# Laying the head norms of queries and keys in phases in a TensorE-bound hybrid layer

## The chip, the cores and the metric

One core of one Trainium2 chip runs one program. The metric is the device time of one execution in microseconds (us); a lower time is better. The kernel before was timed three times: 871.57, 872.2 and 875.5 us, median 872.2.

The engines are named as the profile names them: PE is TensorE (matmuls, with PEld for its weight loads), DVE is VectorE, ACT is ScalarE, POOL is GpSimd, SP is SyncE, which here issues most transfers.

## What is computed

One layer of an encoder with four kinds of heads, on 2048 tokens of width 1024, in float32. All four read one projection of the normed input into eleven slots of 256 columns:

```python
h = rmsnorm(x, norm_g[l])
proj = h @ w_in[l]
a_u, a_v, a_g, b_q, b_k, b_v, b_g, c_in, c_g, d_q, d_g = jnp.split(proj, N_IN_SLOTS, axis=-1)
y_a = chunked_spatial_gating(a_u, a_v, ...) * silu(a_g)
y_b = neighbourhood_attention(b_q, b_k, b_v, ...) * silu(b_g)
y_c = fourier_mixing(c_in, fn_w[l]) * silu(c_g)
mem_n = rmsnorm(mem, mem_norm_g[l])
y_d = memory_attention(d_q, mem_n, mem_w_kv[l], ...) * silu(d_g)
x = x + jnp.concatenate([y_a, y_b, y_c, y_d], axis=-1) @ w_out[l]
```

In both attentions each head of 64 columns of the query and of the key is normed by itself, `q * rsqrt(mean(q*q) + eps)`, before the products. These are the norms of this change. The memory attention reads 256 memory tokens, whose keys and values are projected once.

## The kernel before

**Split products.** Nearly every float32 product is made of three matmuls (L147) on a high and a low half of each operand (`mm3`). The halves of a weight tile, `hilo`, come from a `raw` tile that SP loads: ACT casts the high half (L217, L229), POOL or DVE subtracts it for the low half (L219, L231). In `get_w2` the low half is POOL's for even k and DVE's for odd k.

**Passes.** The 2048 tokens are two halves `h`. `proj` makes one or two slots of a half; `pair` makes two slots side by side (`pair_qk`: queries and keys of the neighbourhood attention, `pair_vv`: the gating's v and the attention's values) in two turns `u`. A turn has four token tiles in four accumulators `acc` of PSUM, and eight steps k of the contraction, 12 matmuls each, 96 in all; the last two steps are taken tile by tile, so that the tiles are complete after 78, 84, 90 and 96. The next turn takes the same four accumulators as they are read out. Weight tiles are held in six buffers, three steps' worth.

**The order.** `drive` counts modelled TensorE time `self.t`; each matmul adds to it. It alternates between the main sequence (the passes, in quanta of three to six matmuls) and tasks that are due, lowest priority number first. A task is a generator; `yield 6.5` means that it is due again 6.5 us of modelled time later. TensorE executes in exactly the order in which this code is run. The other engines' queues are ordered by a scheduler, which goes by the priority that `self.hp(n)` gives to a block of code, and each is executed in order. Tiles come from pools: a tile takes the buffer of an older one once that one's readers are done; the order in which the code asks for tiles decides who gets which. The pool `nat` has five buffers of 128 x 512.

**The norms.** When the accumulators of a query slot are complete, `do_dq` (memory query) or `do_bqk` (queries and keys) is spawned. For each of four tiles `evac_nat` copies from PSUM to a `nat` tile, scaled by the token's norm (L368 DVE, L370 ACT), and `head_norm` squares (L376, ACT), sums per head (L378, DVE), takes the root (`rsqrt`, L124 and L125, POOL) and multiplies (L381, DVE). Then, after the `yield`, `emit_T` transposes the tile on TensorE (L151, `mi<-ident,nat`), splits it and stores it (L419 for the memory query).

**The memory task.** `mem_kv` projects the memory tokens in eight steps of six matmuls into `sc` (`sc<-PT,P`), with `yield 1.5` after each. Behind the eighth it loads the memory rows in four transfers into `nat` tiles (L494), squares them (L495, ACT), takes their root (`rm`, L497 and `rsqrt`), scales keys and values out of PSUM (L502, L505, L507, ACT; L508, DVE), norms the key by `head_norm` and copies it (L513). It runs at the time of the first half's V pass, whose evacuation `evac_vv` (L454 to L463) takes six `nat` tiles a turn and stores four of them to `V` (L463). `bcast` (L302) copies a row of token norms out of a bank that transposes use next.

Of the kernel before, what the change touches and what calls it, by code (L numbers as in the profile page):

```python
# [47 lines left out]
class Kern:  # L48
# [324 lines left out]
    def head_norm(self, q):  # L373
        nc = self.nc
        sq = self.sqp.tile([128, 512], F32, name="sq")
        nc.scalar.activation(out=sq, in_=q, func=AF.Square)  # L376
        ss = self.small.tile([128, 8], F32, name="hss")
        nc.vector.tensor_reduce(out=ss, in_=sq.rearrange("p (g d) -> p g d", d=HD), axis=AX.X, op=ALU.add)  # L378
        self.rsqrt(ss, ss, 1.0 / HD, 8)
        qv = q.rearrange("p (g d) -> p g d", d=HD)  # L380
        nc.vector.tensor_tensor(out=qv, in0=qv, in1=ss.unsqueeze(2).broadcast_to([128, 8, HD]), op=ALU.mult)  # L381
        return q
# [37 lines left out]

    def do_dq(self, h, ps):
        with self.hp(8000):
            qs = [self.head_norm(self.evac_nat(h, [(ps[b][:, j * 256:(j + 1) * 256], 2 * b + j) for j in range(2)]))
                  for b in range(4)]
        yield 6.5 if h else 14.0
        for b in range(4):
            self.emit_T("d", h * 4 + b, [qs[b][:, 0:256], qs[b][:, 256:512]])
            yield 3.3
        self.done.add(f"d_q{h}")

    def do_bqk(self, h, u, ps):
        with self.hp(8000):
            qs = [self.head_norm(self.evac_nat(h, [(ps[t], u * 4 + t)])) for t in range(4)]
        yield 6.5
        for b in range(2):
            for i, kind in ((1, "k"), (0, "q")):
                self.emit_T(kind, h * 4 + u * 2 + b, [qs[2 * b + j][:, i * 256:(i + 1) * 256] for j in range(2)])
                yield 3.3
        if u:
            self.done.add(f"b_qk{h}")  # L440
# [26 lines left out]
    def mem_kv(self):  # L467
        nc, I = self.nc, self.ins
        ps = [self.ps_sc.tile([128, 512], F32, name=self.nsc) for _ in range(2)]
        for k in range(8):  # L470
            with self.hp(0):
                raw = self.att.tile([128, 256], F32, name="dq", bufs=2)
                nc.sync.dma_start(out=raw, in_=I["memT"][k * 128:(k + 1) * 128, :])
                if k % 2 == 0:
                    wraw = self.tabp.tile([128, 2, 512], F32, name="tab")
                    nc.sync.dma_start(out=wraw, in_=I["w_kv"][k * 128:(k + 2) * 128, :].rearrange(
                        "(t p) c -> p t c", t=2))
                m = self.att.tile([128, 2, 256], F32R, name="P", bufs=4)
                nc.scalar.activation(out=m[:, 0], in_=raw, func=AF.Copy, scale=self.gmcol[:, k:k + 1])
                nc.vector.scalar_tensor_tensor(out=m[:, 1], in0=raw, scalar=self.gmcol[:, k:k + 1],  # L480
                                               in1=m[:, 0].bitcast(F32), op0=ALU.mult, op1=ALU.subtract)
                if k % 2 == 0:
                    wt = self.att.tile([128, 2, 2, 512], F32R, name="PT", bufs=2)
                w = [wt[:, k % 2, 0], wt[:, k % 2, 1]]
                self.evac_split(w[0], w[1], wraw[:, k % 2])
            for t in range(2):
                sl = slice(t * 128, t * 128 + 128)
                self.mm3(ps[t], (m[:, 0, sl], m[:, 1, sl]), w, k == 0, k == 7)
            yield 1.5
        ss = self.c([128, 2, 2], "mss")  # L490
        for t in range(2):
            for u in range(2):
                raw = self.nat.tile([128, 512], F32, name="nat")
                nc.sync.dma_start(out=raw, in_=I["mem"][t * 128:(t + 1) * 128, u * 512:(u + 1) * 512])  # L494
                nc.scalar.activation(out=raw, in_=raw, func=AF.Square, accum_out=ss[:, t, u:u + 1])  # L495
        rm = self.c([128, 2], "rm")
        nc.vector.tensor_tensor(out=rm, in0=ss[:, :, 0], in1=ss[:, :, 1], op=ALU.add)  # L497
        self.rsqrt(rm, rm, 1.0 / D, 2)
        q = self.nat.tile([128, 512], F32, name="nat")
        self.vm = self.c([128, 2, 4, 128], "vm", F32R)  # L500
        for t in range(2):
            nc.scalar.activation(out=q[:, t * 256:(t + 1) * 256], in_=ps[t][:, 0:256], func=AF.Copy,  # L502
                                 scale=rm[:, t:t + 1])
            v = self.sqp.tile([128, 256], F32, name="sq")
            nc.scalar.activation(out=v, in_=ps[t][:, 256:512], func=AF.Copy, scale=rm[:, t:t + 1])  # L505
            v4 = v.rearrange("p (h d) -> p h d", d=HD)
            nc.scalar.copy(out=self.vm[:, t, :, 0:HD], in_=v4)  # L507
            nc.vector.tensor_tensor(out=self.vm[:, t, :, HD:2 * HD], in0=v4,  # L508
                                    in1=self.vm[:, t, :, 0:HD].bitcast(F32), op=ALU.subtract)
        self.psum(True)  # L510
        self.head_norm(q)
        twice = self.att.tile([128, 512, 2], F32, name="PT", bufs=2)
        nc.vector.tensor_copy(out=twice, in_=q.unsqueeze(2).broadcast_to([128, 512, 2]))  # L513
        self.spawn(self.mem_k(twice), 20.0)
# [736 lines left out]
```

## Time and profile before

| | before |
|---|---|
| three runs, median (us) | 872.2 (871.57 to 875.5) |
| profiled execution, own time (us) | 872.36 |
| its span (us) | 870.6 |
| mean granted TensorE clock | 0.995 |
| TensorE matmuls busy | 852.1 us, 98% |
| TensorE weight loads busy | 713.6 us, 82% |
| VectorE busy | 502.6 us, 58% |
| ScalarE busy | 407.1 us, 47% |
| GpSimd busy | 327.2 us, 38% |
| bytes moved | 177.88 MB, mean 204 GB/s |

The span is what the profiler saw between the first and the last instruction of one execution; its own time is the device time of that same execution, 1.8 us more. Busy time counts matmuls from start to modelled end, which overlap. In a timeline, a number in brackets is how long the engine had nothing to do before that instruction, and what it waited for. The chain of waits follows the work that ended last back to the start, each step to what released it. The granted clock is a share of TensorE's 2.4 GHz.

### The profile page before, as it was taken

Reading aid. Unit: us, or ns where it says so; the run is one execution under the profiler, and the core shown is the slowest. Engines: PE = TensorE matmul, PEld = TensorE weight load, DVE = VectorE, ACT = ScalarE, POOL = GpSimd, SP = SyncE. Lnnn points to the kernel's source line nnn. Section 1 sums busy time; section 2 is a strip of 40 time slices with the busy share of each in tenths; the row PEclk is TensorE's granted clock in tenths of the full one; section 3 lists DMA queues with packets and bytes.
Section 4 is the critical chain, followed back from the end, with each engine's and each line's share of the span. In section 5 each row is a group of like instructions: output and inputs, shape, how many; then the busy total and the mean of one; then the engine's idle time right before and its main releaser. Section 6 shows DMA issues by size and latency. Waiting matters only on the chain.

```text
span 870.6 us, 13653 instructions
## 1 busy us (share of the span) xinstructions
PE 852.1 (98%) x4448; PEld 713.6 (82%) x4448; DVE 502.6 (58%) x1064; ACT 407.1 (47%) x930; POOL 327.2 (38%) x368
## 2 busy tenths in 40 slices
PE   8999999999999999999999999999999999999998
PEld 7987788888788878887789888888878788888886
DVE  5356565587532557775454866676788777851111
ACT  5674353466632533544324655666765455521110
POOL 1136331155232122552232734434554433235550
PEclk9999999999999999999999999999999999999999
DMA  8967653346762562569669897864598987556661
GB/s 274 323 202 231 191 141 109 117 118 176 227 192 96 187 215 84 142 169 278 210 194 306 265 299 246 263 213 142 175 311 280 320 243 221 174 168 195 205 204 68
DMA packets 147463, 177.88 MB, mean 204 GB/s; under 512 B 29232, under 2 KB 105152, under 8 KB 147392
## 3 DMA queue, kind: packets, MB, share of 16 engines
q1 hardware_dynamic: 145104, 170.33, 62.6%
q0 software_dynamic: 1728, 6.29, 2.5%
q8 instruction: 35, 0.57, 0.3%
q10 hardware_dynamic: 560, 0.40, 0.2%
q14 instruction: 36, 0.29, 0.1%
HBM read 132.92 MB, written 44.05 MB: 203 GB/s over the span
## 4 chain that ended last, share of the span: by engine, by line
PE 78%; DMA 9%; DVE 6%; ACT 3%; issue 2%; POOL 2%; SPq 0%; ACTq 0%; DVEq 0%; POOLq 0%
PE acc L147 60%; PE w L147 8%; PE w L151 4%; PE sc L147 3%; DMA bt<-in_bias 2%; PE mi L147 2%; DMA nat<-in_mem 1%; DMA QD<-st 1%; DMA raw<-in_w_out 1%; DVE PT L535 1%; POOL hss L125 1%; DVE P L916 1%; DMA raw<-in_w_in 1%; DVE hilo L990 1%; DMA nat<-in_x 0%
## 5 line engine op out<-in xcount | busy, mean ns | idle before, releaser
L147 PE MATMUL acc<-hilo 128*128 128x512 f32 (+1 forms) x2880 | 710.5, 390 | 7.6 <-DVE nat L460 1.9
L147 PEld LDWEIGHTS acc<-hilo 128*128 128x128 f32 x2880 | 510.0, 189 | 100.1 <-issue 2.9
L219 POOL TENSOR_TENSOR hilo<-raw,hilo 128x512 fp32r<-128x512 f32 x52 | 68.5, 1319 | 171.2 <-ACT hilo L217 141.5
L231 POOL TENSOR_TENSOR hilo<-raw,hilo 128x512 fp32r<-128x512 f32 x32 | 43.3, 1352 | 114.4 <-ACT hilo L229 93.8
L983 POOL TENSOR_TENSOR nat<-nat 128x256 f32<-128x256 f32 x48 | 36.7, 764 | 93.4 <-DMA nat<-O 61.9
L229 ACT CAST hilo<-raw 128x512 fp32r<-128x512 f32 x64 | 39.7, 621 | 65.9 <-PE acc L147 54.9
L918 ACT ACTIVATE P<-P,smx 128x288 f32<-128x288 f32 (+1 forms) x64 | 39.9, 623 | 54.1 <-DVE smx L916 54.0
L535 DVE TENSOR_TENSOR PT<-w,PT 128x512 fp32r<-128x512 f32 (+2 forms) x96 | 61.2, 637 | 5.6 <-ACT PT L534 5.6
L1027 DVE TENSOR_TENSOR st<-acc,st 128x512 f32<-128x512 f32 (+1 forms) x33 | 21.6, 671 | 70.2 <-PE acc L147 69.9
L989 ACT CAST hilo<-nat 128x256 fp32r<-128x256 f32 x64 | 25.7, 406 | 76.3 <-PE acc L147 57.2
L534 ACT CAST PT<-w 128x512 fp32r<-128x512 f32 (+2 forms) x96 | 52.1, 543 | 18.6 <-PE w L151 18.0
L151 PE MATMUL w<-ident,P 128*128 128x128 f32 (+1 forms) x352 | 54.2, 273 | 1.0 <-DVE smx L916 1.0
L151 PEld LDWEIGHTS w<-ident,P 128*128 128x128 f32 (+1 forms) x352 | 43.0, 135 | 14.6 <-DVE smx L916 1.9
L217 ACT CAST hilo<-raw 128x512 fp32r<-128x512 f32 x51 | 31.3, 618 | 47.9 <-PE acc L147 35.4
L125 POOL TENSOR_TENSOR hss<-hss,mhalf 128x8 f32<-128x8 f32 x25 | 42.7, 1712 | 1.5
L916 DVE CUSTOM_DVE_ANT_0 P<-w,bt 128x288 f32<-128x288 f32 (+1 forms) x64 | 35.6, 556 | 13.2 <-DMA bt<-in_bias 10.3
L231 DVE TENSOR_TENSOR hilo<-raw,hilo 128x512 fp32r<-128x512 f32 x32 | 22.0, 689 | 31.0 <-ACT hilo L229 25.5
L607 ACT ACTIVATE P<-w,smx 128x256 f32<-128x256 f32 x64 | 29.7, 469 | 20.5 <-DVE smx L603 20.2
L958 POOL TENSOR_TENSOR ob<-tmp 64x128 f32<-64x128 f32 x64 | 30.1, 489 | 21.8 <-DVE tmp L954 20.6
L345 DVE TENSOR_TENSOR st<-acc,rbc 128x512 f32<-128x512 f32 x32 | 22.0, 686 | 26.4 <-PE acc L147 23.5
L138 DVE SCALAR_TENSOR_TENSOR hilo<-raw,gcol,hilo 128x512 fp32r<-128x512 f32 x32 | 26.2, 829 | 17.5 <-ACT hilo L137 16.6
L921 DVE TENSOR_SCALAR P<-P,smx 128x288 f32<-128x288 f32 (+1 forms) x64 | 34.0, 531 | 1.8
(170 smaller groups left out, 1062.7 us busy)
## 6 DMA issues: line engine op xcount, KB each, us to landing
raw<-in_w_in SPq DMA_DIRECT2D x119, 256.0 KB, 3.1
raw<-in_xT SPq DMA_DIRECT2D x32, 256.0 KB, 3.8
nat<-in_x SPq DMA_DIRECT2D x32, 256.0 KB, 5.3
G<-st SPq DMA_DIRECT2D x32, 256.0 KB, 3.4
nat<-G SPq DMA_DIRECT2D x64, 128.0 KB, 2.8
st<-in_x SPq DMA_DIRECT2D x32, 256.0 KB, 4.9
out_y<-st SPq DMA_DIRECT2D x31, 256.0 KB, 3.3
tab<-in_dft_s POOLq DMA_DIRECT2D x12, 512.0 KB, 5.2
```

What stands on the lines that cost most here:

```text
L125: nc.gpsimd.tensor_tensor(out=out, in0=out, in1=self.mhalf[:, :n], op=ALU.pow)
L147: self.nc.tensor.matmul(out=out, lhsT=lhsT, rhs=rhs, start=start, stop=stop, **k)
L151: self.nc.tensor.transpose(out=out, in_=in_, identity=self.ident)
L219: eng.tensor_tensor(out=w[1], in0=raw, in1=w[0].bitcast(F32), op=ALU.subtract)
L229: nc.scalar.copy(out=w[0], in_=raw)
L231: eng.tensor_tensor(out=w[1], in0=raw, in1=w[0].bitcast(F32), op=ALU.subtract)
L534: self.nc.scalar.copy(out=hi, in_=src)
L535: (eng or self.nc.vector).tensor_tensor(out=lo, in0=src, in1=hi.bitcast(F32), op=ALU.subtract)
L916: nc.vector.tensor_tensor_reduce(out=P[:, :n], in0=sc[:, :n], in1=bt[:, :n], op0=ALU.add, op1=ALU.min, scale=-1.0, scalar=3e38, accum_out= ...
L918: nc.scalar.activation(out=P[:, :n], in_=P[:, :n], func=AF.Exp, bias=sm[:, 1:2], scale=-1.0, accum_out=sm[:, 2:3])
L921: nc.vector.tensor_scalar(out=P[:, :n], in0=P[:, :n], scalar1=sm[:, 3:4], scalar2=None, op0=ALU.mult)
L983: mul.tensor_tensor(out=g, in0=o, in1=g, op=ALU.mult)
```

## The change

`head_norm` ends after the root and returns it; the multiplication is a function of its own, `scale_norm`. `do_dq` and `do_bqk` first evacuate four tiles, then make four sums and roots, wait 2.5 us of modelled time, make the four multiplications, and wait 4.5 us more (12.0 for the first memory query). The two waits sum to 7.0 and 14.5, where one wait of 6.5 and 14.0 stood. `mem_kv` calls the two functions one after the other. No instruction is added or removed. Line numbers behind the change are 4 higher from the multiplication on and 14 higher from `evac_vv` on (L494 becomes L508, L495 becomes L509).

```diff
@@ -377,6 +377,10 @@
         ss = self.small.tile([128, 8], F32, name="hss")
         nc.vector.tensor_reduce(out=ss, in_=sq.rearrange("p (g d) -> p g d", d=HD), axis=AX.X, op=ALU.add)
         self.rsqrt(ss, ss, 1.0 / HD, 8)
+        return ss
+
+    def scale_norm(self, q, ss):
+        nc = self.nc
         qv = q.rearrange("p (g d) -> p g d", d=HD)
         nc.vector.tensor_tensor(out=qv, in0=qv, in1=ss.unsqueeze(2).broadcast_to([128, 8, HD]), op=ALU.mult)
         return q
@@ -420,9 +424,14 @@
 
     def do_dq(self, h, ps):
         with self.hp(8000):
-            qs = [self.head_norm(self.evac_nat(h, [(ps[b][:, j * 256:(j + 1) * 256], 2 * b + j) for j in range(2)]))
+            qs = [self.evac_nat(h, [(ps[b][:, j * 256:(j + 1) * 256], 2 * b + j) for j in range(2)])
                   for b in range(4)]
-        yield 6.5 if h else 14.0
+            ss = [self.head_norm(q) for q in qs]
+        yield 2.5
+        with self.hp(8000):
+            for q, s in zip(qs, ss):
+                self.scale_norm(q, s)
+        yield 4.5 if h else 12.0
         for b in range(4):
             self.emit_T("d", h * 4 + b, [qs[b][:, 0:256], qs[b][:, 256:512]])
             yield 3.3
@@ -430,8 +439,13 @@
 
     def do_bqk(self, h, u, ps):
         with self.hp(8000):
-            qs = [self.head_norm(self.evac_nat(h, [(ps[t], u * 4 + t)])) for t in range(4)]
-        yield 6.5
+            qs = [self.evac_nat(h, [(ps[t], u * 4 + t)]) for t in range(4)]
+            ss = [self.head_norm(q) for q in qs]
+        yield 2.5
+        with self.hp(8000):
+            for q, s in zip(qs, ss):
+                self.scale_norm(q, s)
+        yield 4.5
         for b in range(2):
             for i, kind in ((1, "k"), (0, "q")):
                 self.emit_T(kind, h * 4 + u * 2 + b, [qs[2 * b + j][:, i * 256:(i + 1) * 256] for j in range(2)])
@@ -508,7 +522,7 @@
             nc.vector.tensor_tensor(out=self.vm[:, t, :, HD:2 * HD], in0=v4,
                                     in1=self.vm[:, t, :, 0:HD].bitcast(F32), op=ALU.subtract)
         self.psum(True)
-        self.head_norm(q)
+        self.scale_norm(q, self.head_norm(q))
         twice = self.att.tile([128, 512, 2], F32, name="PT", bufs=2)
         nc.vector.tensor_copy(out=twice, in_=q.unsqueeze(2).broadcast_to([128, 512, 2]))
         self.spawn(self.mem_k(twice), 20.0)
```

The order of the instructions moves in three places that matter below. The first is TensorE's queue near the end of the first turn of the first V pass; before:

```order
L147 MATMUL sc<-PT,P 128x512 x6
L147 MATMUL mi<-wsT,st 64x128 x4
L147 MATMUL acc<-hilo 128x512 x3
L147 MATMUL sc<-PT,P 128x512 x6
L151 MATMUL mi<-ident,nat 128x128 x4
L147 MATMUL acc<-hilo 128x512 x6
L147 MATMUL sc<-PT,P 128x512 x6
L147 MATMUL acc<-hilo 128x512 x45
```

and with the change:

```order
L147 MATMUL sc<-PT,P 128x512 x6
L147 MATMUL acc<-hilo 128x512 x12
L151 MATMUL mi<-ident,nat 128x128 x4
L147 MATMUL sc<-PT,P 128x512 x6
L147 MATMUL acc<-hilo 128x512 x12
L147 MATMUL sc<-PT,P 128x512 x6
L147 MATMUL acc<-hilo 128x512 x27
```

The memory task's last step (the last `sc<-PT,P`) stood ahead of 24 matmuls of this turn and the next turn's first ones; now it stands ahead of the turn's last six and the first 21 of the next. The transposes of the memory query (`mi<-ident,nat`) moved back by twelve matmuls.

The second is SP's queue, with the memory loads into `nat` and their neighbours; before:

```order
L494 DMA nat_1046<-in_mem 128x512
L227 DMA raw_1027<-in_w_in 128x2x256
L227 DMA raw_1126<-in_w_in 128x2x256
L494 DMA nat_1049<-in_mem 128x512
L494 DMA nat_1052<-in_mem 128x512
L227 DMA raw_1162<-in_w_in 128x2x256
L473 DMA dq_975<-in_memT 128x256
L494 DMA nat_1055<-in_mem 128x512
```

and with the change, where `nat_1059` to `nat_1075` are V tiles:

```order
L477 DMA V_118<-nat_1059 128x4x128
L423 DMA QD_117<-st_1005 256x1x256
L477 DMA V_118<-nat_1064 128x4x128
L477 DMA V_118<-nat_1070 128x4x128
L227 DMA raw_1282<-in_w_in 128x2x256
L508 DMA nat_1111<-in_mem 128x512
L508 DMA nat_1114<-in_mem 128x512
L227 DMA raw_1288<-in_w_in 128x2x256
L477 DMA V_118<-nat_1075 128x4x128
L508 DMA nat_1117<-in_mem 128x512
L207 DMA raw_1373<-in_w_in 128x2x256
L508 DMA nat_1120<-in_mem 128x512
```

The memory loads stood between weight loads, ahead of every V store, and used one buffer in turn. Now the first two stand behind three V stores and use the buffers of `nat_1064` and `nat_1070`; the third and the fourth use these same two again.

The third is ACT's queue at the squares of the memory rows; before:

```order
L495 ACTIVATE nat_1052,mss_1045<-nat_1052 128x512
L229 CAST hilo_933<-raw_931 128x512
L479 ACTIVATE P_979<-dq_975,gmcol_149 128x256
L495 ACTIVATE nat_1055,mss_1045<-nat_1055 128x512
L534 CAST st_854<-mi_849 128x512
L229 CAST hilo_1023<-raw_1021 128x512
L302 ACTIVATE sa_o_865<-mi_863 8x128
```

and with the change, where `hilo_1248` is the high half of the next turn's weights for k = 4:

```order
L509 ACTIVATE nat_1111,mss_1110<-nat_1111 128x512
L509 ACTIVATE nat_1114,mss_1110<-nat_1114 128x512
L509 ACTIVATE nat_1117,mss_1110<-nat_1117 128x512
L509 ACTIVATE nat_1120,mss_1110<-nat_1120 128x512
L516 ACTIVATE nat_1127<-sc_769,rm_1123 128x256
L519 ACTIVATE sq_1130<-sc_769,rm_1123 128x256
L516 ACTIVATE nat_1127<-sc_770,rm_1123 128x256
L519 ACTIVATE sq_1135<-sc_770,rm_1123 128x256
L521 CAST vm_1128<-sq_1130 128x4x64
L521 CAST vm_1128<-sq_1135 128x4x64
L376 ACTIVATE sq_1144<-nat_1127 128x512
L229 CAST hilo_1248<-raw_1246 128x512
```

The four squares stood apart, with casts of weights and of the memory projection between them. Now they stand in one run with the six operations that read the memory projection and the key's square, and the cast of the weights for k = 4 is behind them all.

## Rows read from the trace of the kernel before

**Rows 1.** Page, part 1: busy time, share of the span, instructions of each engine.

```profile
PE 852.1 (98%) x4448; PEld 713.6 (82%) x4448; DVE 502.6 (58%) x1064; ACT 407.1 (47%) x930; POOL 327.2 (38%) x368
```

**Rows 2.** Chain of waits, two pieces: start us, us, what.

```profile
134.03 2.78 PE acc L147 x12
...
237.86 65.35 PE acc L147 x288
```

**Rows 3.** Windows: us; busy us (count) per engine; granted clock, DMA share, GB/s.

```profile
97.10:100.60 3.50, 3.50 (x10) 2.73 (x9) 2.49 (x7) 0.62 (x1) 1.86 (x3) 0.51 0.59 157
650.00:654.00 4.00, 2.47 (x13) 1.82 (x12) 2.52 (x7) 3.57 (x9) 1.83 (x2) 1.00 0.90 293
```

**Rows 4.** Waits of TensorE: line, releaser: us in total, times, longest.

```profile
PE acc L147 <- DVE nat L460: 1.9, 3, 1.3
```

**Rows 5.** Timeline of TensorE, 75 to 105 us: start us, us, instruction [idle before <-releaser].

```profile
75.13 0.66 PE L151 MATMUL mi<-ident,nat 128*128 128x128 f32 x4 [1.78 <-ACT sa_o L302]
...
83.80 0.60 PE L151 MATMUL mi<-ident,nat 128*128 128x128 f32 x4
84.15 1.62 PE L147 MATMUL acc<-hilo 128*128 128x512 f32 x6
85.61 1.55 PE L147 MATMUL sc<-PT,P 128*128 128x512 f32 x6
87.00 7.00 PE L147 MATMUL acc<-hilo 128*128 128x512 f32 x30
95.28 0.96 PE L147 MATMUL acc<-hilo 128*128 128x512 f32 x3 [1.27 <-DVE nat L460]
96.69 4.58 PE L147 MATMUL acc<-hilo 128*128 128x512 f32 x12 [0.45 <-DVE nat L460]
101.20 1.09 PE L147 MATMUL w<-wsT,nat 128*64 128x128 f32 x16
102.22 2.36 PE L147 MATMUL acc<-hilo 128*128 128x512 f32 x9
```

**Rows 6.** Timeline of TensorE at 235 us.

```profile
235.29 0.71 PE L147 MATMUL w<-PT,vm 128*128 128x256 f32 x4 [1.26 <-DVE st L407]
```

**Rows 7.** Timeline of GpSimd, 75 to 93 us.

```profile
75.18 1.28 POOL L231 TENSOR_TENSOR hilo<-raw,hilo 128x512 fp32r<-128x512 f32 x1
...
91.42 1.67 POOL L125 TENSOR_TENSOR hss<-hss,mhalf 128x8 f32<-128x8 f32 x1
```

**Rows 8.** Timeline of ScalarE, 65 to 95 us.

```profile
65.64 0.63 ACT L495 ACTIVATE nat<-nat 128x512 f32<-128x512 f32 x1 [2.72 <-DMA nat<-in_mem]
...
74.82 0.26 ACT L302 ACTIVATE sa_o<-mi 8x128 f32<-8x128 f32 x1
...
86.58 0.47 ACT L502 ACTIVATE nat<-sc,rm 128x256 f32<-128x256 f32 x1
...
88.62 0.50 ACT L456 ACTIVATE nat<-acc,rstd 128x256 f32<-128x256 f32 x1
...
94.23 0.47 ACT L459 ACTIVATE nat<-acc,rstd 128x256 fp32r<-128x256 f32 x1 [1.79 <-DMA V<-nat]
```

**Rows 9.** Chain of waits, 60 to 95 us: its transfers.

```profile
60.72 4.84 DMA nat<-in_mem
...
66.39 3.07 DMA nat<-in_mem
...
70.29 2.83 DMA nat<-in_mem
...
90.20 3.94 DMA V<-nat
```

**Rows 10.** DMA issues, 54 to 125 us: count, KB each, median us to landing.

```profile
V<-nat SPq DMA_DIRECT2D x7, 256.0 KB, 2.8
```

**Rows 11.** Timeline of VectorE, 73 to 92 us.

```profile
73.96 0.16 DVE L497 TENSOR_TENSOR rm<-mss 128x2 f32<-128x2 f32 x1 [1.37 <-ACT nat L495]
...
90.37 0.68 DVE L378 TENSOR_REDUCE hss<-sq 128x8 f32<-128x512 f32 x1
```

## The prediction

> **What bounds the kernel.** I read the engine totals first: TensorE is busy for 852.1 of 870.6 us, so anything gained or lost has to come out of the 18.5 us in which it is idle, or out of its clock [rows 1]. The chain of waits says the same: in one of its longest pieces 288 projection matmuls run back to back for 65.35 us, 227 ns each [rows 2]. That stretch is full; no order of the norms makes it shorter. The Trainium skill's page "Perfetto Trace Analysis" (section "Identifying the Most-Contended Engine") warns that busy time of matmuls says little and that the share of weight loads is the one to look at. By that, 18% of the span would be room; with the full stretch as the measure, only idle time and lost clock are.
>
> So the question is which halts of TensorE the change touches. The table of what TensorE waited for gives them by releaser; its top row is 1.9 us in three waits [rows 4]. The timeline places those near a norm: 1.78 us at 75.13, 1.27 at 95.28, 0.45 at 96.69 [rows 5] and 1.26 at 235.29 [rows 6]. The second and third are followed by the only other loss there: from 97.10 to 100.60 the granted clock is 0.51, about 1.2 instead of 2.4 GHz, and twelve matmuls take 4.58 us where twelve elsewhere take 2.78 [rows 2, 3, 5].
>
> **The change, part by part.**
>
> *What is added or removed.* Nothing: the same squares, sums, roots and multiplications, on the same engines and tiles. The sum is about order alone.
>
> *Phases inside a norm.* A root on GpSimd takes 1.67 us for its power alone [rows 7], a square 0.63 on ScalarE [rows 8]. Laying four evacuations, then four sums, keeps ScalarE from waiting on a root between two squares. But each engine's queue is ordered by the scheduler, not by the code, and TensorE next needs these tiles several microseconds later. I cost the phases themselves at nothing; what hides them is the projection that runs between, which cannot go away: the yields still hold TensorE's transposes back.
>
> *The yields.* They sum to 7.0 and 14.5 instead of 6.5 and 14.0. The transposes therefore stand some 0.5 us of modelled TensorE time later, which shifts every task with a lower priority that waits for the same slots. The order of TensorE shows what follows at one place above all: the last step of the memory projection (six matmuls into sc) stood after 72 of the 96 matmuls of the first half of the V pass; now it stands after 90. With it the code behind that step moves, memory loads, their squares, the root and the key's norm: it was written before the evacuation of the V pass and is now written after it. The four loads took a `nat` buffer before the V tiles did; now they take two buffers that V tiles hold until their stores have landed.
>
> *What goes (gain).* Before, the four memory loads follow each other through one buffer: 4.84, 3.07 and 2.83 us are on the chain [rows 9]. ScalarE stands in its queue before each one's square, 2.72 us for the second, and L302, which frees the bank that the halt at 75.13 waits for, stands behind the fourth [rows 8]. With the memory block moved away, this halt goes: 1.78. The rest of the block (86.58 to 88.62 on ScalarE) stood just ahead of the V pass's first evacuation [rows 8], and after it a V store of 3.94 us held a buffer [rows 9], for which ScalarE waited 1.79 at 94.23 [rows 8]. So TensorE got its accumulators late: 1.27 and 0.45. With the block gone and two sc steps of 1.39 us [rows 5] now between the V tiles, these go too, and with them the slow clock: 4.58 - 2.78 = 1.80. Together 1.78 + 1.27 + 0.45 + 1.80 = **5.3 us**.
>
> *What comes (loss).* On ScalarE the four squares, six small operations and the key's square now stand in one run ahead of the cast of the weights for k = 4 of the second half; on GpSimd both roots stand ahead of their low half. Count from the moment the first V tile is complete. TensorE needs the weights after a set of transposes (0.35), an sc step (1.39), twelve matmuls (2.78), another sc step (1.39), six matmuls (1.39), 48 matmuls (4 x 2.78 = 11.12) and two groups of mixing (1.02 each): 20.5 us [rows 2, 5]. The weights come so: the third V tile is complete at 4.52; its evacuation to the issue of its store takes 1.58 (88.62 to 90.20) [rows 8, 9]; the store 2.8 to 3.94 [rows 9, 10]; then a load, its square (0.75, from 65.64 to the next load at 66.39 [rows 8, 9]), a second load and its square; then the root of the memory rows 1.22 (73.96 to the instruction behind it at 75.18), six operations on ScalarE 2.04 (86.58 to 88.62), a square 0.63, a sum 0.68, a root 2.04 (from the sum's end at 91.05 to 93.09), the low half 1.28 [rows 7, 8, 11], and an estimated 0.5 for hand-offs of about 0.1: 8.39. With a store of 2.8 and two loads of 3.07 that is 4.52 + 1.58 + 2.8 + 6.14 + 1.50 + 8.39 = 24.93, so a new halt of 4.5 us. With loads of 2.83 it is 4.0; with a store of 3.94 and loads of 4.84 it is 9.2. I take 4.5, since two of the three loads are near it.
>
> *What stands behind the waiting loads.* On SyncE the fourth V store, one weight load and the next slot's weights follow the loads that wait for the second and third V store. The store is issued at about 9 us of the same count and lands by 13, before the memory key needs its buffer (16.5); the weight load is for k = 7, used 8 us after those of k = 4. Both are covered. The transposes of the memory queries move too, with their evacuations and eight stores, by two quanta of 1.39 at most; the product that reads them comes behind the whole V pass, whose second half has over 11 us of matmuls, so nothing.
>
> The Trainium skill's page "DMA: Bandwidth & Descriptors" (section "Anatomy of one DMA") gives some 2.0 us plus the bytes at 436 GB/s for a transfer on the GpSimd path, an estimate of 2.6 us for these 256 KB. By it the halt would be 3.4 and the sum 1.1 us lower. These transfers are issued by SyncE in the midst of others, and none of the three loads was that short [rows 9]; the rows decide.
>
> *Clock after the new halt.* Two bounds: 1.5 us of idle time between 650 and 654 left the clock at 1.00 [rows 3], so 0; the 1.27 and 0.45 at 95 us cost 1.80. The new halt is longer than either and lies in the same pass: I take 1.80, and 3.6 as the worst.
>
> *The other norms.* For the first key and query norm of half 0 the order before its stall of 1.26 at 235.29 [rows 6] keeps the same distance: nothing, with a bound of 1.5 on either side (the stall gone, or doubled with little over). In half 1 and at the second memory query no wait for a norm is among the larger ones; the same row bounds them, and I take nothing.
>
> *Sum.* -5.3 + 4.5 + 1.8 = **+1.0 us** on the profiled execution's 872.36, 873.4. The median of the runs shown, 872.2, is 0.16 lower, so 873.2.
>
> **The rivals.**
>
> *The memory chain is longer than the cover (slower).* The one mechanism is the new place of the loads: in line behind V stores on SyncE, two after two through two buffers. For it: the first load took 4.84 us and the V store 3.94 in just such company [rows 9]. Against it: the others took about 3. The halt is then up to 9.2, with clock 1.8 to 3.6: 872.2 - 5.3 + 9.2 + 1.8 to 3.6 = 877.9 to 879.7. It turns slower than the bound below from a store and two loads of some 12.1 us together (my sum has 8.94: a halt 3.2 longer, 7.7, with 1.8 to 2 of clock).
>
> *The gains stay and the new wait does not bind (faster).* The old halts go, and the weights arrive nearly in time because the scheduler's stores and loads overlap better than my single file: 872.2 - 5.3 + 0.5 = 867.4. For it: all three halts have a clear cause that moves. Against it: it needs the store and both loads within 5 us, against at least 8.5 in the rows.
>
> *The change does little.* Before, the evacuations of the first memory query already stood together, with the sums behind, so phases alone move nothing; if the move of the memory block also cancels out, the time is 872.2.
>
> **How the numbers follow.** The forecast's own case (old halts gone, a new one of about its size) has 0.49, with 869 to 876.6 as its own range; the longer chain 0.25; the gain that stays 0.16; little change 0.10. Faster or slower counts from 0.5%, 4.4 us, about what a measurement of this kernel tells from no change: so below 867.8 and above 876.6. Faster 0.16, same 0.49 + 0.10 = 0.59, slower 0.25. The range reaches from 867.0, just under the second rival, to 880.0, just over the first's worst.
>
> **What would show it.** Right: in the profile after, TensorE has no halt behind L302 or the V tiles (now L474) between 70 and 100 us; ScalarE's first memory square (L509) comes after the V evacuations and waits for its load; one halt of 4 to 5 us behind a low half (L231) lies some 20 us after the first V tile, with a stretch of clock at about half behind it. Wrong: no such halt, or one over 8 us; a slow clock at both places; or a new halt over 2 us at the key and query norms.

## The result and the profile after

| | before | with the change |
|---|---|---|
| median of four runs on one chip (us) | 871.94 (871.57 to 875.5) | 882.23 (880.35 to 884.73) |
| profiled execution, own time (us) | 872.36 | 882.35 |
| its span (us) | 870.6 | 880.2 |
| TensorE matmuls busy (us) | 852.1 | 853.8 |

The ratio is 1.0097, with a 95% interval of 1.0072 to 1.0122: the change makes the kernel slower by about 1%, 10 us between the two profiled executions. The forecast was 873.2 with a range to 880.

The busy time, which answers to [rows 1], shows the same work: 4448 matmuls in both. The table of what TensorE waited for (line, releaser: us in total, times, longest) has a new first row. Nothing like it stood before, where the first row was 1.9 us in three waits [rows 4]:

```profile
PE w L147 <- ACT sq L519: 10.4, 1, 10.4
PE acc L147 <- DVE nat L474: 1.6, 2, 1.4
```

One single wait is 10.4 us. The timeline of TensorE at the end of the first turn of the V pass answers to [rows 5]:

```profile
84.08 0.60 PE L151 MATMUL mi<-ident,nat 128*128 128x128 f32 x4
...
88.66 1.55 PE L147 MATMUL sc<-PT,P 128*128 128x512 f32 x6
...
95.10 3.01 PE L147 MATMUL acc<-hilo 128*128 128x512 f32 x12 [1.45 <-DVE nat L474]
108.46 1.97 PE L147 MATMUL w<-wsT,nat 128*64 128x128 f32 x16 [10.36 <-ACT sq L519]
110.36 3.53 PE L147 MATMUL acc<-hilo 128*128 128x512 f32 x9
113.82 1.09 PE L147 MATMUL w<-wsT,nat 128*64 128x128 f32 x16
```

The wait stands at 108.46, at the first mixing of the gating (`w<-wsT,nat`), not at a projection matmul. The halt of 1.78 at 75.13 [rows 5] has gone, as forecast. The halt behind the V tiles has not: it is 1.45 at 95.10, in place of 1.27 and 0.45. The clock by windows (busy us and count per engine, then granted clock, DMA share, GB/s), which answers to [rows 3]:

```profile
94.00:98.20 4.20, 3.01 (x12) 2.17 (x12) 1.82 (x4) 1.05 (x2) 0.45 (x1) 1.00 0.91 252
98.20:108.40 10.20, 0.00 (x0) 0.00 (x0) 0.16 (x1) 3.64 (x11) 0.89 (x2) 0.72 0.50 151
108.40:114.80 6.40, 6.34 (x41) 4.96 (x41) 3.72 (x6) 2.58 (x7) 3.08 (x3) 0.64 0.12 41
```

The clock stayed at 1.00 around the halt of 1.45 and was low after the long one: the 16 matmuls of the mixing took 1.97 us instead of 1.09, and the nine of the projection behind them 3.53 instead of 2.36 [rows 5]. The sum near the memory task is then 10.36 + 0.88 + 1.17 new, 1.45 instead of 1.72 behind the V tiles, and 1.78 and the 1.80 of slow clock gone: +8.6 of the 9.6 us between the two spans. Compared at points where both kernels have done the same matmuls, TensorE is 0.98 us behind the kernel before at 62.7 us and 9.35 behind at 118.7, so this stretch makes 8.4 of the 9.6. The 0.98 was lost in the first 15 us, where the profiles of the other runs lie between -0.18 and 1.52; whether the change has a part in it is not shown. The small waits further on about cancel.

What TensorE waited for stands in the chain of waits (start us, us, what):

```profile
91.62 3.81 DMA V<-nat
...
95.45 3.69 DMA nat<-in_mem
...
99.24 0.73 ACT nat L509 x2
...
100.38 0.43 SPq L207
...
100.86 4.62 DMA nat<-in_mem
...
105.56 0.09 ACT nat L509
...
106.84 0.71 POOL rm L125
...
107.57 0.47 ACT nat L516
108.04 0.37 ACT sq L519
```

A V store of 3.81 us, a memory load of 3.69, its square, a weight load that SyncE issued in between, a second load of 4.62, its square, the root, and two reads of the first bank of the memory projection (L516 for the keys, L519 for the values). Then the mixing starts, 0.04 us later.

The mixing's own data had long been there; VectorE's last operation on them in this turn (L688) ended at 95.60:

```profile
94.87 0.73 DVE L688 TENSOR_SCALAR nat<-nat,sa 128x256 f32<-128x256 f32 x2
```

So the mixing does not wait for data: it waits for a PSUM bank. Behind the last memory step `mem_kv` closes the two small pools and opens a common one of four banks (`self.psum(True)`, tiles named `w`); the first mixing of the gating takes a bank of it that still holds the memory projection, and L516 and L519 can't read that out before the root of the memory rows is known. Run 6 tests this.

### The profile page after: what moved, and what is told of

Read it like the earlier page. It is cut to its first block, busy times and chain, and to the rows that moved or that the text cites. A ratio compares the mean times of both kernels' runs of the same rounds, so it can differ in the third digit from the quotient of the medians.

```text
span 880.2 us, 13652 instructions
## 1 busy us (share of the span) xinstructions
PE 853.8 (97%) x4448; PEld 715.8 (81%) x4448; DVE 497.9 (57%) x1064; ACT 408.5 (46%) x930; POOL 329.6 (37%) x368
## 4 chain that ended last, share of the span: by engine, by line
PE 81%; DMA 8%; DVE 5%; ACT 2%; POOL 2%; issue 2%; SPq 0%; ACTq 0%; DVEq 0%; POOLq 0%
PE acc L147 61%; PE w L147 9%; PE w L151 4%; PE sc L147 4%; PE mi L147 2%; DMA bt<-in_bias 2%; DMA raw<-in_xT 1%; DMA nat<-in_mem 1%; DMA O<-z 1%; DMA G<-st 1%; POOL hss L125 1%; PE mi L151 1%; DMA raw<-in_w_in 1%; DVE PT L549 1%; POOL hilo L219 1%
## 5 line engine op out<-in xcount | busy, mean ns | idle before, releaser
L219 POOL TENSOR_TENSOR hilo<-raw,hilo 128x512 fp32r<-128x512 f32 x52 | 69.9, 1347 | 166.8 <-ACT hilo L217 143.2
L231 POOL TENSOR_TENSOR hilo<-raw,hilo 128x512 fp32r<-128x512 f32 x32 | 44.4, 1389 | 114.2 <-ACT hilo L229 92.8
L229 ACT CAST hilo<-raw 128x512 fp32r<-128x512 f32 x64 | 39.8, 621 | 58.9 <-PE acc L147 49.4
L972 POOL TENSOR_TENSOR ob<-tmp 64x128 f32<-64x128 f32 x64 | 30.2, 490 | 21.7 <-DVE tmp L968 20.5
```

Source lines behind the costliest of these rows:

```text
L219: eng.tensor_tensor(out=w[1], in0=raw, in1=w[0].bitcast(F32), op=ALU.subtract)
L229: nc.scalar.copy(out=w[0], in_=raw)
L231: eng.tensor_tensor(out=w[1], in0=raw, in1=w[0].bitcast(F32), op=ALU.subtract)
```

## The experiments

In their comparisons the kernel before had medians of 874.3 to 875.0. The expectations name times against 872; what counts is the ratio to the kernel before in the same comparison, which is given with its interval. A profile shows one execution, and single executions of one kernel differ by several us (871.67 to 879.2 in run 1); it tells where the halts stand, not by how much the median moved. Where a profile is said to be ahead or behind, it is at the same matmul.

**1. Phases kept, old sums of the waits.**

```diff
-        yield 4.5 if h else 12.0
+        yield 4.0 if h else 11.5
...
-        yield 4.5
+        yield 4.0
```

> The phases stay, the two waits sum to the old 6.5 and 14.0 (4.0 and 11.5 behind the multiplications instead of 4.5 and 12.0), so TensorE's order is that of the kernel before. Theory (the half microsecond moved the memory block behind the V evacuation, and the mixing waits for its banks): 872 within 1.5, no halt behind L519, the old halts of 1.8 (behind L302) and 1.3 plus 0.5 (behind the V tiles) are back, with slow clock after them. Rival (the phases and the late multiplications cost the time): 880 to 882, with a halt of several us near 100 still there.

Measured: ratio 1.0008 (0.9985 to 1.0031), the level of the kernel before. TensorE's timeline has the old halts back, and no wait at the mixing:

```profile
75.19 0.66 PE L151 MATMUL mi<-ident,nat 128*128 128x128 f32 x4 [1.49 <-ACT sa_o L302]
...
95.77 0.96 PE L147 MATMUL acc<-hilo 128*128 128x512 f32 x3 [1.70 <-DVE nat L474]
97.96 4.58 PE L147 MATMUL acc<-hilo 128*128 128x512 f32 x12 [1.23 <-DVE nat L474]
```

The phases and the late multiplications as such cost nothing that can be measured.

**2. No phases, only the longer waits.**

```diff
-        yield 6.5 if h else 14.0
+        yield 7.0 if h else 14.5
...
-        yield 6.5
+        yield 7.0
```

> The code of before with its single waits set to 7.0 and 14.5: no phases, but TensorE's order is that of the change. Theory: 882 within 2, one halt of 9 to 11.5 us at the first mixing, behind the ACT line that reads the memory projection (L505). Rival (the phases cost it): 872, no such halt.

Measured: ratio 1.0078 (1.0054 to 1.0102). The wait table has the same row as with the change, at the line that this kernel has for it:

```profile
PE w L147 <- ACT sq L505: 10.9, 1, 10.9
```

The halt is as expected; the time, 878.8 on the scale of the expectation, is a little under its 880 to 884. The half microsecond alone makes the loss: the interval overlaps that of the change.

**3. Only the first memory query's wait set back.**

```diff
-        yield 4.5 if h else 12.0
+        yield 4.5 if h else 11.5
```

> The change with the wait of the first memory query alone set back (2.5 + 11.5 = 14.0); queries and keys keep 2.5 + 4.5 = 7.0. Theory (the half microsecond of this one wait is the cause): at the level of the kernel before within 0.3%, the memory loads ahead of the V stores, no halt behind L519. Rival (the half microsecond at the queries and keys has a share): slower than before by 0.3 to 1%.

Measured: ratio 1.0013 (0.9987 to 1.0040), no halt at the mixing, the old ones back:

```profile
75.95 0.66 PE L151 MATMUL mi<-ident,nat 128*128 128x128 f32 x4 [1.67 <-ACT sa_o L302]
...
96.56 0.98 PE L147 MATMUL acc<-hilo 128*128 128x512 f32 x3 [1.74 <-DVE nat L474]
97.97 4.58 PE L147 MATMUL acc<-hilo 128*128 128x512 f32 x12 [0.43 <-DVE nat L474]
```

So the 0.5 us that count are those of one wait, of the first memory query. The other waits have no share that the ratio shows. In the trace they have a small one: a set of transposes in the second half waits 1.55 us at 401.14 for L411, which reads out keys, as with the change (1.51 at 406.51), and neither before nor in run 1.

**4. The change, with the memory loads written ahead of the memory steps.** The block from `ss = self.c([128, 2, 2], "mss")` to the root of `rm` moves, unchanged, from behind the loop over k in `mem_kv` to ahead of it.

> The change, with the four memory loads, their squares and their root written ahead of the eight memory steps instead of behind them; TensorE's order is that of the change. Theory: the root is ready when the last memory step ends at about 90, the banks are read by 93, and the halt of 10.4 and the slow clock behind it (2.3) go: 869.5 if nothing comes back, 872 if the halt of 1.8 behind L302 returns with the loads. Rival (the step's new place in TensorE's order is itself what costs): 880 or more, the mixing still waits over 5 us.

Measured: ratio 0.9963 (0.9941 to 0.9984), faster than the kernel before. TensorE's order is the change's, but the memory loads are the 63rd, 66th, 67th and 70th transfer in SyncE's queue, where the kernel before had 63, 66, 67 and 70 too and the change has 94, 95, 98 and 100. The mixing at 99.12 waits for nothing:

```profile
75.80 0.66 PE L151 MATMUL mi<-ident,nat 128*128 128x128 f32 x4 [0.57 <-ACT sa_o L302]
...
96.21 2.98 PE L147 MATMUL acc<-hilo 128*128 128x512 f32 x12 [1.58 <-DVE nat L474]
99.12 1.09 PE L147 MATMUL w<-wsT,nat 128*64 128x128 f32 x16
```

What remains is 0.57 behind L302 and 1.58 behind the V tiles, with no slow clock. Against the kernel before that is 5.30 - 2.15 = 3.15 us less in this stretch, 0.36%, close to the ratio. The profiled execution as a whole does not confirm it: it took 873.74 us, 1.4 more than the profiled one before. It is 2.1 us ahead of it at 118.7 and 1.3 behind at the end; its longest halt of all, 2.05, stands at 395.55. The place of the last memory step in TensorE's order is not what costs. Whether that place brings the gain is not shown, since no run has early loads with the step in its old place.

**5. The same early loads without the phases** (single waits of 7.0 and 14.5).

> As the kernel with the loads written early, but with single waits of 7.0 and 14.5 and no phases: the same order of TensorE and ScalarE. Theory (phases are worth nothing either way): the same time within 0.3%. Rival (the phases bring the 0.4% that the version with early loads was below the kernel before): slower than that version by 0.3% or more, at the level of the kernel before.

Measured: ratio 0.9964 (0.9948 to 0.9979), the same as with the phases. In its profile the halt behind L302 is long, with slow clock behind it (0.86 from 72 to 84 us), and the one behind the V tiles absent:

```profile
78.41 0.66 PE L151 MATMUL mi<-ident,nat 128*128 128x128 f32 x4 [3.57 <-ACT sa_o L302]
```

This profile is not ahead of the kernel before at the mixing (101.82 against 101.20), though the ratio is that of run 4: the halts of one execution do not account for the median to within 3 us. By the ratios the phases are a second time worth nothing either way.

**6. The change, with the bank's readers freed of the root.**

```diff
-                                 scale=rm[:, t:t + 1])
+                                 scale=1.0)
...
-            nc.scalar.activation(out=v, in_=ps[t][:, 256:512], func=AF.Copy, scale=rm[:, t:t + 1])
+            nc.scalar.activation(out=v, in_=ps[t][:, 256:512], func=AF.Copy, scale=1.0)
```

> The change, leaving out the factor of the memory rows' root in keys and values (scale 1.0): the readers of the two banks need no load any more, but by the order of ScalarE they still stand behind the squares of the first pair of loads, ahead of the second pair. Theory: the mixing still waits, until about 101.5 instead of 108.4, so a halt of 3 to 4 us in place of 10.4, and little or no slow clock: 873 to 876. Rival (the bank is not what the mixing waits for): 880 or more.

Measured: ratio 1.0032 (1.0015 to 1.0050), which is 874.8 on the scale of the expectation. TensorE and ScalarE:

```profile
101.71 1.38 PE L147 MATMUL w<-wsT,nat 128*64 128x128 f32 x16 [3.79 <-ACT sq L519]
103.03 3.62 PE L147 MATMUL acc<-hilo 128*128 128x512 f32 x9
```

```profile
99.02 0.63 ACT L509 ACTIVATE nat<-nat 128x512 f32<-128x512 f32 x1 [0.17 <-ACT nat L509]
...
101.00 0.38 ACT L516 ACTIVATE nat<-sc 128x256 f32<-128x256 f32 x1 [1.26 <-DMA V<-nat]
101.28 0.38 ACT L519 ACTIVATE sq<-sc 128x256 f32<-128x256 f32 x1
```

The mixing starts 0.05 us after the first bank's second reader (101.28 + 0.38), which now stands behind one pair of squares instead of both, and the halt is 3.79 instead of 10.36. What the readers waited for last is no square either: L516 stood 1.26 us for a V store, since the keys' tile that it writes takes a `nat` buffer too. The mixing follows its bank's reader, at 108.41 in the change and at 101.66 here: this is the bank, shown by moving its reader. Only "little or no slow clock" was missed: the 3.8 us halt was followed by one.

```profile
97.90:101.70 3.80, 0.02 (x1) 0.00 (x0) 0.00 (x0) 2.14 (x7) 0.00 (x0) 1.00 0.91 218
101.70:107.60 5.90, 5.89 (x42) 4.39 (x42) 2.30 (x6) 3.47 (x10) 1.52 (x3) 0.71 0.39 139
```

**7. The mixing put later.** The first turn's mixing is due 16 us behind its evacuation.

```diff
-        yield 4.0
+        yield 4.0 if h or u else 16.0
```

> The change, with the first turn's mixing due 16 instead of 4 us after its V evacuation, so that it comes behind 63 more matmuls; the memory loads stay where the change put them. Theory: the bank is not the only thing behind the memory chain. The mixing no longer waits, but the low half of the weights for k = 4 (L231), which by the profile of the change ends at about 114.6 while TensorE would ask for it at about 104.5, takes its place with a halt of 8 to 10 us: 880 to 883. Rival (only the banks bind; the weights are in time within the 4.5 us of my forecast): 869 to 876.

Measured: ratio 1.0031 (1.0008 to 1.0055), 874.7 on that scale: the rival's range, and a miss for the theory. The long wait has gone; TensorE waits 0.22, 0.85 and 0.50 us (and 0.17) for weights behind those for k = 4, not 8 to 10:

```profile
94.27 12.21 PE L147 MATMUL acc<-hilo 128*128 128x512 f32 x52 [0.78 <-DVE nat L474]
106.70 2.80 PE L147 MATMUL acc<-hilo 128*128 128x512 f32 x11 [0.22 <-DVE hilo L231]
...
111.02 0.98 PE L147 MATMUL acc<-hilo 128*128 128x512 f32 x3 [0.85 <-POOL hilo L231]
112.50 0.73 PE L147 MATMUL acc<-hilo 128*128 128x512 f32 x2 [0.50 <-DVE hilo L231]
...
127.67 1.66 PE L147 MATMUL acc<-hilo 128*128 128x512 f32 x6 [2.31 <-DVE nat L474]
```

The weights for k = 4 were there without a wait, and the reason is in ScalarE's queue: the scheduler, given another order of TensorE, put their cast (L229) between the two pairs of squares, where the change had the four squares in one run.

```profile
98.27 0.63 ACT L509 ACTIVATE nat<-nat 128x512 f32<-128x512 f32 x1 [2.60 <-DMA nat<-in_mem]
...
99.54 0.60 ACT L229 CAST hilo<-raw 128x512 fp32r<-128x512 f32 x1
103.35 0.63 ACT L509 ACTIVATE nat<-nat 128x512 f32<-128x512 f32 x1 [3.20 <-DMA nat<-in_mem]
```

So this run shows that the halt goes with the mixing's place, but not what the weights for k = 4 would have done in the change's own order; that stays open. The 2.31 at 127.67 is a price of the late mixing: VectorE multiplies the mixing's result (L698) ahead of the next V tiles in its queue, and stood there for the store of an earlier one:

```profile
122.16 0.48 DVE L698 SCALAR_TENSOR_TENSOR sa_o<-w,lng,bias 128x256 f32<-128x256 f32 x1 [2.77 <-DMA O<-sa_o]
```

**8. Two buffers for the memory rows alone, in the change.**

```diff
-                raw = self.nat.tile([128, 512], F32, name="nat")
+                raw = self.memp.tile([128, 512], F32, name="nat")
...
+        self.memp = P("memp", 2, ef)
```

> The change with the memory rows in two buffers of their own; TensorE's order is that of the change, the loads and squares now stand among the first of their queues, far ahead of the V pass. Theory (the halt is the way memory buffer, load, square, root, bank): the mixing waits under 1 us, no halt behind L302, only the V tiles' 1.5 is left: 867 to 870, faster than before by 0.2 to 0.6%. Rival (the new place of the last memory step costs by itself, whatever the loads do): 878 or more. A third way: the four loads now collide with the full stream of the first 40 us and the gain is eaten there: 872 to 876.

Measured: ratio 0.9964 (0.9949 to 0.9980), 868.9 on the scale of the expectation and in its theory's range. The halt at the mixing and those at 75 and 95 us are gone; 27 matmuls run through to the mixing:

```profile
63.24 1.86 PE L147 MATMUL sc<-PT,P 128*128 128x512 f32 x6 [1.80 <-DVE nat L368]
...
93.81 6.67 PE L147 MATMUL acc<-hilo 128*128 128x512 f32 x27
100.41 1.09 PE L147 MATMUL w<-wsT,nat 128*64 128x128 f32 x16
```

But a new halt of 1.80 stands at 63.24, with slow clock behind it. The loads, now free to go, are the 27th, 30th, 36th and 53rd transfer in SyncE's queue instead of the 94th to 100th, ahead of the loads of the tokens that the norms are made from and among them. VectorE's row for the token norms, before and now, and the window from 55 to 75 us:

```profile
54.00 0.17 DVE L293 TENSOR_TENSOR rstd<-ss 128x8 f32<-128x8 f32 x1 [7.42 <-ACT nat L291]
59.15 0.17 DVE L293 TENSOR_TENSOR rstd<-ss 128x8 f32<-128x8 f32 x1 [0.46 <-ACT nat L291]
```

```profile
55.00:75.00 20.00, 18.20 (x78) 14.60 (x77) 11.84 (x22) 12.28 (x27) 13.92 (x14) 0.91 0.30 81
```

The norms of the tokens come at 59.15, where they came at 54.00 before, and the clock is 0.91 over the window. This halt is the third way of the expectation, in part; that the early loads make it is borne out by run 10, which holds them back.

**9. The same two buffers in the kernel before.**

> The kernel before with the same two buffers. Theory (with loads out of the way the memory step's place matters only through ScalarE's six operations ahead of the V evacuation): the halt of 1.8 behind L302 goes, the halts of 1.3 and 0.5 behind the V tiles and the slow clock (1.8) stay or shrink: 868.5 to 871, some 1 to 3 us above the change with own buffers. Rival (the phases cost something where nothing covers it): below the change with own buffers.

Measured: ratio 0.9981 (0.9968 to 0.9994), 870.3 on the scale of the expectation and in its range. The figure lies between the kernel before and run 8, but the intervals of runs 8 and 9 overlap, so no difference between them is shown. The halt at 75 is gone, those behind the V tiles stay, without slow clock. The new halt of run 8 is here too, which the expectation did not have:

```profile
62.34 2.02 PE L147 MATMUL sc<-PT,P 128*128 128x512 f32 x6 [1.80 <-DVE nat L368]
...
96.88 0.98 PE L147 MATMUL acc<-hilo 128*128 128x512 f32 x3 [1.02 <-DVE nat L460]
98.29 2.98 PE L147 MATMUL acc<-hilo 128*128 128x512 f32 x12 [0.43 <-DVE nat L460]
```

The clock is 0.72 from 62 to 68 us, so in this profile the new halt takes back what the old one gave: at 123.7 it is 0.05 us ahead of the kernel before.

**10. Own buffers, the first pair of loads held until the token norms are there.**

```diff
+                if t == 0:
+                    nc.vector.tensor_copy(out=raw[:, 0:1], in_=self.rstd[0][:, 0:1])
```

> The change with two buffers of their own for the memory rows, the first pair of loads held back until the first half's token norms are there (two copies of one column on VectorE). Theory: the loads stand between the token statistics (which they delayed by some 5 us when free, with a halt of 1.8 at 63 and slow clock behind it) and the V pass; no halt over 1 us between 55 and 75 us nor at the mixing, at most the V tiles' 1.5 us near 95: 868 to 871, 0.4 to 0.7% below the kernel before. Rival (any place of the loads costs about the same): 872 to 873, as the other two versions with the loads out of the way.

Measured: ratio 0.9984 (0.9963 to 1.0005), not the 0.4 to 0.7% forecast, and not clear of no difference. The token norms come at 55.52 and the halt at 63 is gone, but the one behind the V tiles is longer than the 1.5 forecast:

```profile
75.83 0.66 PE L151 MATMUL mi<-ident,nat 128*128 128x128 f32 x4 [0.28 <-ACT sa_o L302]
...
98.03 2.96 PE L147 MATMUL acc<-hilo 128*128 128x512 f32 x12 [2.37 <-DVE nat L474]
```

By the chain of waits a V store of 3.52 us, issued at 93.27, held ScalarE's evacuation until 96.90; why it was issued no earlier was not followed up. This did not improve on the versions of 4, 5 and 8, which are the best seen, 0.36% below the kernel before.

## Why the prediction was wrong

*What is added; the phases.* Right: worth nothing. Runs 1, 5 and, from the other side, 2 show it.

*The yields.* Right, and all of the matter: the longer wait of the first memory query moves the last memory step from 72 to 90 of the 96 matmuls, the memory block behind the V evacuation, and its loads behind V stores. Run 3 pins it to that one wait, but for the 1.5 us halt behind L411 in the second half.

*What goes.* 5.3 us were to go. The 1.78 and the slow clock of 1.80 went; the two halts behind the V tiles shrank only from 1.72 to 1.45. So 3.85 of 5.3. The V tiles wait for their own stores (ScalarE stood 1.94 us for one at 93.96), not for the memory block alone, as the step had it.

*What comes.* This is the step that failed: "TensorE needs the weights". The first thing behind the memory chain that TensorE needs is not the weights for k = 4, after 20.5 us, but the bank for the mixing. It comes 21 matmuls into the next turn: by my own terms 7.30 + 21 x 0.232 = 12.2 us after the first V tile. The reader of the bank stood in the very rows that I quoted, ScalarE's L516 and L519 out of `sc`, and the line `self.psum(True)` in the code next to them; I read them as a queue ahead of a cast and did not ask who waits for what they free. With my terms up to the end of the first L519 (4.52 + 1.58 + 2.8 + 6.14 + 1.50 + 1.22 + some 0.9 for the two reads together, 18.7 in all) the halt would have been 6.5 and the forecast 875, still inside "same"; with the upper rows for the store and both loads (3.94 and 4.84), 11.2 and 879.9.

The second part of the error is in the same step, the length of the chain: measured from 84.08 it ended at 108.41, 24.3 us instead of 18.7. Less the 12.2 us of matmuls and the halt of 1.45 on the way, that leaves 10.7, where 10.36 was measured. The third tile was complete at 88.66, as counted; the stores that free the loads' buffers were issued 2.96 us later (from 91.62 on) instead of 1.58, since SyncE had a weight load and three other stores ahead of them; the store took 3.81 instead of 2.8, the loads 3.69 and 4.62 instead of 3.07 each, and 0.9 went between the first square and the second load (99.97 to 100.86), with a weight load in SyncE's queue. I had taken the middle of the rows for transfers that I had myself put into the busiest stretch; the upper bound (3.94 and 4.84) was close to what came. By the Trainium skill's page "DMA: Bandwidth & Descriptors" (section "Anatomy of one DMA") each would be an estimate of 2.6 us; its fit is for another path, and the loads of 3.69 and 4.62 here decide.

*The clock.* The price of 1.80 was close: 0.88 + 1.17 = 2.05. That slow clock would follow this halt was right; that none followed the one of 1.45 shows in the window at 94 us.

*The other norms.* About nothing, as taken: the stall of 1.26 at 235 went, one of 1.51 came at 406 behind L411, in the second half, where the step had taken nothing with a bound of 1.5.

*The rivals.* The mechanism of the first one came true, the loads in line behind V stores; its top of 879.7 was too low because it, too, counted to the weights. One of the signs that it gave for being wrong, a halt of over 8 us, is what the profile has. The second, that the gains stay, is what runs 4, 5 and 8 look like once the loads are taken out of the line. The chance for slower, 0.25, was too small: the loss was worked out for one waiting point alone, and an earlier one could only add to it.

## What to carry to other kernels

When a block of work moves later, list everything that it frees (buffers and PSUM banks, also through a change of pools) and everyone who takes that next, and price the wait at the earliest of them, not at the one that is nearest in the queue that you happen to look at. Where a change moves transfers into a stretch that is busy, take their durations from the upper rows. And a wait written in code that also sets an order is not a small number: half a microsecond moved a block that holds the bank for 13 us from its first load on (95.45 to 108.41), while the edit that the change was about did nothing; changing the two apart, as runs 1 and 2 do, shows that with two runs.

## What had not been expected

Freed loads can be too early: with buffers of their own the memory rows went among the first transfers and made the token norms 5 us late (run 8; its expectation had named a collision there, but not this path). And the granted clock did not fall around a halt of 1.45 us, while as a mean it was 0.71 in the 5.9 us after a halt of 3.79 and 0.64 in the 6.4 us after one of 10.36. The length of the halt alone does not tell it: around halts of 2.31 (run 7, 122 to 132 us) and 2.37 (run 10, 94 to 104 us) the clock was 1.00, while after the 1.80 of run 8 it was 0.67 from 63.2 to 68.4 us.
